# A two-block transformer kernel on one core: SBUF tiles of 1 KB and more moved to one byte offset, and the latents' squares added ahead of their sums

## The chip, the cores and the metric

The kernel runs on one core of a Trainium2 chip, as one program. The metric is the device time of one execution in microseconds (us). Before the change three runs took 1204.91, 1205.18 and 1206.57 us; the median is 1205.18 us.

## The reference, cut to what matters

256 tokens of width 1024, batch 1, all in float32, pass through two blocks one after the other:

```python
# first block
h = h + gated_deltanet(rmsnorm(h))            # 16 value heads of 128, chunks of 64
h = h + conv_gated_mlp(rmsnorm(h))            # "ffn 0": 1024 -> 2*2816 -> 1024
h = h + sliding_window_sink_attention(...)    # 16 heads of 64, window 128
h = h + conv_gated_mlp(rmsnorm(h))            # "ffn 1"
x = rmsnorm(h)
# second block, the "mixer" and "ffn 2"
proj = rms_norm(x) @ w_in
h_q, h_k, h_v, h_g, h_a, c_q, c_kv, k_pe = split(proj)
y_a = gla_branch(h_q, h_k, h_v, h_g, h_a) @ w_o_gla        # gated linear attention
y_b = mla_branch(rms_norm(c_q), rms_norm(c_kv), k_pe) @ w_o_mla   # latent attention
x = x + rms_norm((g_a * y_a + g_b * y_b) @ w_out)
x = x + rms_norm((silu(h @ w_gate) * (h @ w_up)) @ w_down)
```

In the mixer c_kv has 256 and c_q 384 columns; both are called latents here. Each is scaled by the reciprocal root of its mean square, so the sum of its squares over the columns is needed. The gate of gla_branch is log_sigmoid(h_a @ w_a2 + b), summed along the time of a chunk.

## The kernel before, in words

**A product in three parts.** Activations lie transposed in SBUF: 128 features on the partitions, 256 tokens along the free axis, so that one tile of 128 features is 1 KB in a partition. For float32 accuracy every operand is split into a rounded part and a remainder ("hi" and "lo"; in the names `xh` and `xl`, `wh` and `wl`). `mm3` (L248 to L252) makes a product of three matmuls: hi by hi (L250), lo by hi (L251), hi by lo (L252). In `gemm` the weights are stationary (128 x 128) and the activations stream past (256 columns, 1 KB a partition). In `gemm_nat`, and in the last product of ffn 2, it is the other way round: 128 tokens of an activation are stationary and 512 columns of the weights stream (2 KB a partition). In a row of the profile the operand ahead of the comma streams and the one behind it is stationary: `pb<-xh,wh` streams `xh`.

**Weights.** All weights lie in one array in the order in which they are used, in chunks of 128 x 1024. `w` (L231) hands out tiles of 128 columns; for each chunk `_prep` (L176) starts the DMA into `wr`, lets ScalarE round it into `wh` (L187) and VectorE subtract that to give `wl` (L188). One chunk feeds 24 matmuls that stream 256 columns.

**Order.** The program is written out by Python generators. A stage that is waiting for other engines is a "side" generator; each group of four weight tiles gives every side one step (`tick`), and `yield` puts off what follows by one step. So a number of yields is a distance in weight tiles between two pieces of a stage. The engines work through their queues in order.

**Where tiles lie.** Pools are laid one behind the other in a partition: constants, the weight pool `wp` (four buffers each of wr, wh, wl), `h`, the small pool `sp`, then `xp` with the pair xh, xl, then pools of the single stages. Within a pool tiles follow one another as they are first asked for, so that a tile begins where the small tiles ahead of it happen to end.

**The latents in the mixer.** `lat` (L1336) splits one of the five latent tiles and squares it on ScalarE (L1342) into a buffer `sql[i]`. `lat_stage` (L1431) waits until the two squares of c_kv exist, yields three times, adds them on VectorE (L1436), and at once issues the sum over the partitions (`colsum`, L367, a matmul with a column of ones); from that comes the scale `rkv`, which `rows` (L453, `rowp`) spreads over the partitions. For c_q it does the same with three squares (L1444, L1445), three yields and a second colsum. `la_stage` (L1391) runs beside it: it turns the rotary key (L1381, `rot`), makes the gate (L1404, in two halves), its logarithm on ScalarE (L1409 to L1411) and its running sum on VectorE (L1413 to L1421). `evac_kd` (L1460) scales the keys and multiplies them by that (L1467); their transposes stand on TensorE (L1473, `kdt`).

Of the kernel before, what the change touches and what calls it, by code (L numbers as in the profile page):

```python
# [2 lines left out]

# [1 line left out]

# [4 lines left out]
F32 = mybir.dt.float32  # L10
F32R = mybir.dt.float32r
BF16 = mybir.dt.bfloat16
I32 = mybir.dt.int32
AF = mybir.ActivationFunctionType
ALU = mybir.AluOpType
# [4 lines left out]
P = 128  # L20
# [87 lines left out]

CW = _cw_terms()

WARM = (5, 1, 3)
# [29 lines left out]
class Builder:  # L143
# [413 lines left out]
    def run(self):  # L557
        nc, tc = self.nc, self.tc
        with ExitStack() as es:
            self.cp = es.enter_context(tc.tile_pool(name="cp", bufs=1))  # L560
            self.wp = es.enter_context(tc.tile_pool(name="wp", bufs=2))
            self.hp = es.enter_context(tc.tile_pool(name="hp", bufs=1))
            self.sp = es.enter_context(tc.tile_pool(name="sp", bufs=2))
            self.xp = es.enter_context(tc.tile_pool(name="xp", bufs=1))
            self.dp = es.enter_context(tc.tile_pool(name="dp", bufs=1, space=DRAM))
            self.ps = es.enter_context(tc.tile_pool(name="ps", bufs=8, space=PSUM))
            self.h = self.hp.tile([P, KD, T], F32, name="h")
            self.cols = self.cp.tile([P, NCOL], F32, name="cols")
            self.ident = self.cp.tile([P, P], F32, name="ident")
            for b in range(4):  # L570
                nc.sync.dma_start(self.h[:, 2 * b : 2 * b + 2], self.a["xT"][:, 2 * b : 2 * b + 2])
            nc.sync.dma_start(self.ident, self.cst("ident"))
            self._raw(0)
            nc.sync.dma_start(self.cols, self.a["cols"])
            self.ones = self.cp.tile([P, P], F32, name="ones")
            nc.gpsimd.memset(self.ones, 1.0)
            self.gdn()
            if self.upto < 2:
                return
            with tc.tile_pool(name="xp2", bufs=1) as self.xp2:  # L580
                self.ffn(0)
                if self.upto < 3:
                    return
                self.swa()
            if self.upto < 4:
                return
            with tc.tile_pool(name="lp", bufs=1) as self.lp:
                self.block2_consts()
                self.ffn(1)
                if self.upto < 5:  # L590
                    return
                self.block2()
# [6 lines left out]
    def gdn(self):  # L599
        nc, tc, sp = self.nc, self.tc, self.sp  # L600
        x = self.newx()
        self.sqs = []
        with tc.tile_pool(name="gp", bufs=1) as gp:

            wb = self.bank("warm")
            warm = lambda n, r: [nc.tensor.matmul(wb[:, 0 : r.shape[1]], self.ones, r, start=True, stop=True) for _ in range(n)]
            warm(WARM[0], self.ones)
            for b in range(4):
                self.add_sq(self.sqs, "sqa", b, lambda o: nc.scalar.activation(o, self.h[:, 2 * b : 2 * b + 2], AF.Square))
            cs = self.colsum(self.sqs)  # L610
            if PRE0:
                self._prep(0)
            rc = self.rstd(cs, D)
            warm(WARM[1], self.sqs[0])
            rb = self.rows(rc, psum=True)
            warm(WARM[2], self.h[:, 0])
            for i in range(8):
                t = gp.tile([P, T], F32, tag="t2", bufs=8, name="xn")
                op = nc.vector.scalar_tensor_tensor(t, self.h[:, i], self.col("a_norm", i), rb, ALU.mult, ALU.mult)
                nc.scalar.activation(x[0][:, i], t, AF.Copy)  # L620
                nc.vector.tensor_tensor(x[1][:, i], t, x[0][:, i].bitcast(F32), ALU.subtract)  # L621
                if i in PINS:
                    self.pins[PINS[i]] = op
                    self._prep(PINS[i])
            self.gdn_body(gp, x)
# [407 lines left out]
    def ffn(self, layer):  # L1033
        nc, tc, sp = self.nc, self.tc, self.sp
        x = self.x
        self.stats_rows(D)
        with tc.tile_pool(name=f"fp{layer}", bufs=1) as fp:
            padded = [fp.tile([P, 2, 2 + T], F32, tag=f"fpad{i}", name=f"fpad{i}") for i in range(3)]
            for t in padded:
                nc.gpsimd.memset(t[:, :, 0:2], 0.0)  # L1040
            acts = {}
            self.side(self.bias_rows(fp) if layer == 0 else self.rope_tables(fp))

            def evac(g, bank):
                u = padded[g % 3]
                nc.vector.tensor_tensor(u[:, :, 2:], bank.rearrange("p (a t) -> p a t", a=2), self.bc2(self.rb), ALU.mult)
                y = fp.tile([P, 2, T], F32, tag="fy", bufs=2, name="fy")
                for i in range(2):
                    ct = g + NFF * i
                    w = lambda j: self.col(f"fcw{layer}", ct * 3 + j)  # L1050
                    nc.scalar.activation(y[:, i], u[:, i, 2:], AF.Identity, bias=self.col(f"fcb{layer}", ct), scale=w(2))
                    for j in range(2):
                        nc.vector.scalar_tensor_tensor(y[:, i], u[:, i, j : j + T], w(j), y[:, i], ALU.mult, ALU.add)  # L1053
                nc.scalar.activation(y[:, 0], y[:, 0], AF.Silu)
                nc.vector.tensor_tensor(y[:, 1], y[:, 1], y[:, 0], ALU.mult)
                ah = fp.tile([P, T], F32R, tag="ah", bufs=LAG + 1, name="ah")
                al = fp.tile([P, T], F32R, tag="al", bufs=LAG + 1, name="al")
                self.split(ah, al, y[:, 1])
                acts[g] = (ah, al)

            cts = []
            for g in range(NFF):
                cts += [g, g + NFF]
            self.acc_started = None
            up = self.gemm(f"w_up{layer}", x, KD, cts, evac, ko=KO[layer])
            for g in range(NFF):
                next(up)
                if g >= LAG and g - LAG not in acts:
                    self.settle()
                if g == LAG - 1:  # L1070
                    self.acc_open()
                if g >= LAG:
                    self.acc_k(f"w_dn{layer}", g - LAG, acts.pop(g - LAG))
            ks = list(range(NFF - LAG, NFF))
            if layer == 0:
                xa, xb = self.newx(), self.newx(tag="f", pool=self.xp2)
                self.x = (xa, xb)
                ev = self.boundary_evac([(xa, self.col("kvn", 0, 8)), (xb, self.col("bn", 0, 8))])
            else:
                wfp = self.sp.tile([P, 8], F32, tag="wfp", bufs=1, name="wfp")  # L1080
                nc.vector.tensor_tensor(wfp, self.col("fin", 0, 8), self.col("prem", 0, 8), ALU.mult)
                xa = self.newx(tag="x")
                self.x = xa
                ev = self.boundary_evac([(xa, wfp)], self.col("fin", 0, 8))
            self.acc_last(f"w_dn{layer}", ks, [acts.pop(k) for k in ks], ev)
        self.out_dbg(f"hf{layer}", self.h)
# [17 lines left out]
    def swa(self):  # L1104
        nc, tc, sp = self.nc, self.tc, self.sp
        xk, xq = self.x
        self.stats(D)
        with tc.tile_pool(name="sw", bufs=1) as ap:
            self.swa_body(ap, xk, xq)

    def swa_body(self, ap, xk, xq):
# [137 lines left out]

    def block2(self):  # L1250
        nc, tc, sp = self.nc, self.tc, self.sp
        with tc.tile_pool(name="mp", bufs=1) as mp:
            xm = self.mixer(mp)
        self.ffn2(xm)

# [34 lines left out]
    def mixer(self, mp):  # L1290
        nc, sp = self.nc, self.sp
# [41 lines left out]
        sql = [None] * 5  # L1333
# [97 lines left out]
        def lat_stage():  # L1431
            while sql[1] is None:
                yield
            for _ in range(3):
                yield
            nc.vector.tensor_tensor(sql[0], sql[0], sql[1], ALU.add)  # L1436
            c = self.colsum(sql[0:1])
            nc.vector.tensor_tensor(rkv, self.rstd(c, 256, rc), rc, ALU.mult)
            yield
# [3 lines left out]
                yield  # L1443
            nc.vector.tensor_tensor(sql[2], sql[2], sql[3], ALU.add)  # L1444
            nc.vector.tensor_tensor(sql[2], sql[2], sql[4], ALU.add)  # L1445
            for _ in range(3):
                yield
            c = self.colsum(sql[2:3])
            nc.vector.scalar_tensor_tensor(rqs, self.rstd(c, 384, rc), 192 ** -0.5, rc, ALU.mult, ALU.mult)
# [1 line left out]

        self.side(la_stage())
        self.side(lat_stage())
        list(self.gemm("w_c", x, KD, [4, 0, 1, 2], evac_c))

# [284 lines left out]
    def ffn2(self, xm):  # L1740
        nc, tc, sp = self.nc, self.tc, self.sp
        stt = nc.vector.scalar_tensor_tensor
        with tc.tile_pool(name="f2", bufs=1) as fp:
            wrow = fp.tile([P, 2, D], F32, tag="wrow", name="wrow")
            nc.gpsimd.dma_start(wrow, self.a["wrow"].to_broadcast([P, 2, D]))
            mw = fp.tile([P, 2, D], F32, tag="mw", name="mw")
# [269 lines left out]
```

## Time and profile before

| | |
|---|---|
| runs, us | 1204.91, 1205.18, 1206.57; median 1205.18 |
| the profiled execution, us | 1206.04 |
| its span, first to last instruction, us | 1204.2 |
| mean granted TensorE clock | 0.99 |
| TensorE matmuls busy | 1166.8 us, 97% of the span, 9308 instructions |
| TensorE weight loads busy | 1102.7 us, 92% |
| VectorE busy | 896.5 us, 74% |
| ScalarE busy | 689.4 us, 57% |
| DMA | 206.00 MB, 171 GB/s on average |

The profiled execution took 1206.04 us, 1.8 us more than its span of instructions. PE in the profile is TensorE at its matmuls and PEld at its weight loads; DVE is VectorE, ACT ScalarE. The ends of matmuls are modelled and overlap, so that the length of one matmul (0.28 us here) is no measure of its price; the distance from one start to the next is.

### The profile page before, as it was taken

The page shows a single profiled execution, that of the slowest core. Times are in us where ns is not written, and L with a number is a line of the kernel's source. Part 1 is how long each engine was busy: PE and PEld are TensorE (multiplying, and loading weights), DVE is VectorE, ACT ScalarE, POOL GpSimd, SP SyncE. Part 2 cuts the span into 40 slices and gives each one's busy share as a digit, 9 for nine tenths or more (in the row PEclk, how much of TensorE's full clock was granted, in tenths as well). Part 3 has the DMA queues.
Part 4 walks back from the last instruction along what each step waited for, and adds up shares of the span by engine and source line. Part 5 has one row for each costly group of instructions (what it writes and reads, how often), then busy time and mean ns, then how long its engine had stood idle before and what let it go on. Part 6 is the DMA issues. An engine that isn't in the chain of part 4 may idle for free.

```text
span 1204.2 us, 23264 instructions
## 1 busy us (share of the span) xinstructions
PE 1166.8 (97%) x9308; PEld 1102.7 (92%) x9308; DVE 896.5 (74%) x1645; ACT 689.4 (57%) x1172; POOL 24.7 (2%) x46
## 2 busy tenths in 40 slices
PE   6999999999999999989999999799999999999997
PEld 6989888999999999889999998689789998999996
DVE  5968977669877879879987879546666667665565
ACT  4786556546655556656655557546465555444443
POOL 2000000000000001000000000000000000000000
PEclk9999999999999999999999999799999999999999
DMA  6546375455665657435656555244245664566562
GB/s 211 191 134 202 120 224 179 140 164 164 218 191 190 187 189 244 132 101 172 196 190 192 183 186 177 70 156 142 88 150 184 192 216 153 174 191 188 185 192 86
DMA packets 68204, 206.00 MB, mean 171 GB/s; under 512 B 18085, under 2 KB 18229, under 8 KB 67840
## 3 DMA queue, kind: packets, MB, share of 16 engines
q1 hardware_dynamic: 65488, 194.77, 51.3%
q0 software_dynamic: 2608, 9.75, 2.3%
q8 instruction: 73, 1.20, 0.4%
q14 instruction: 35, 0.29, 0.1%
HBM read 199.75 MB, written 4.74 MB: 170 GB/s over the span
## 4 chain that ended last, share of the span: by engine, by line
PE 81%; DVE 11%; ACT 3%; issue 2%; DMA 1%; SPq 0%; DVEq 0%; ACTq 0%; POOLq 0%
PE pb L250 18%; PE pb L251 18%; PE pb L252 18%; PE acc L250 6%; PE acc L252 6%; PE acc L251 6%; DVE wl L188 3%; DVE cy L705 1%; DMA NT<-s 1%; DVE TI L817 1%; DVE fst L815 1%; ACT wh L187 0%; DMA ident<-cst 0%; ACT S L1178 0%; DVE fy L1053 0%
## 5 line engine op out<-in xcount | busy, mean ns | idle before, releaser
L188 DVE TENSOR_TENSOR wl<-wr,wh 128x1024 fp32r<-128x1024 f32 x362 | 441.9, 1223 | 193.7 <-ACT wh L187 192.8
L187 ACT ACTIVATE wh<-wr 128x1024 fp32r<-128x1024 f32 x362 | 381.7, 1057 | 319.6 <-issue 88.2
L250 PE MATMUL pb<-xh,wh 128*128 128x256 f32 x1224 | 346.4, 283 | 0.6 <-ACT xh L620 0.6
L251 PE MATMUL pb<-xl,wh 128*128 128x256 f32 x1224 | 343.1, 280 | 0.3 <-DVE xl L621 0.2
L252 PE MATMUL pb<-xh,wl 128*128 128x256 f32 x1224 | 342.8, 281 | 0.2 <-DVE wl L188 0.2
L250 PEld LDWEIGHTS pb<-xh,wh 128*128 128x128 f32 x1224 | 231.2, 189 | 3.1 <-issue 1.6
L251 PEld LDWEIGHTS pb<-xl,wh 128*128 128x128 f32 x1224 | 231.3, 189 | 0.9 <-DVE xl L621 0.4
L252 PEld LDWEIGHTS pb<-xh,wl 128*128 128x128 f32 x1224 | 231.0, 189 | 0.4 <-DVE wl L188 0.4
L250 PE MATMUL pb<-fh,wh 128*128 128x256 f32 x416 | 116.9, 282 | 0.0
L251 PE MATMUL pb<-fl,wh 128*128 128x256 f32 x416 | 116.1, 279 | 0.5 <-DVE fl L471 0.4
L252 PE MATMUL pb<-fh,wl 128*128 128x256 f32 x416 | 115.8, 279 | 0.0
L252 PE MATMUL acc<-ah,wl 128*128 128x256 f32 x352 | 98.1, 279 | 0.4 <-DVE wl L188 0.4
L251 PE MATMUL acc<-al,wh 128*128 128x256 f32 x352 | 98.2, 279 | 0.0
L250 PE MATMUL acc<-ah,wh 128*128 128x256 f32 x352 | 98.1, 279 | 0.0
L251 PEld LDWEIGHTS pb<-fl,wh 128*128 128x128 f32 x416 | 78.3, 188 | 1.5 <-DVE fl L471 0.8
L250 PEld LDWEIGHTS pb<-fh,wh 128*128 128x128 f32 x416 | 78.1, 188 | 1.3 <-issue 0.4
L252 PEld LDWEIGHTS pb<-fh,wl 128*128 128x128 f32 x416 | 78.2, 188 | 0.0
L1053 DVE SCALAR_TENSOR_TENSOR fy<-fpad,cols,fy 128x256 f32<-128x256 f32 x176 | 73.4, 478 | 0.0
L250 PE MATMUL pb<-wh,xh 128*128 128x512 f32 (+1 forms) x176 | 70.9, 405 | 0.0
L251 PE MATMUL pb<-wl,xh 128*128 128x512 f32 (+1 forms) x176 | 68.9, 391 | 1.5 <-DVE wl L188 1.5
L252 PE MATMUL pb<-wh,xl 128*128 128x512 f32 (+1 forms) x176 | 68.5, 389 | 0.0
L252 PEld LDWEIGHTS acc<-ah,wl 128*128 128x128 f32 x352 | 66.2, 188 | 0.6 <-DVE wl L188 0.6
(455 smaller groups left out, 2082.0 us busy)
## 6 DMA issues: line engine op xcount, KB each, us to landing
wr<-wall SPq DMA_DIRECT2D x362, 512.0 KB, 3.8
wzd<-zt POOLq DMA_DIRECT2D x8, 256.0 KB, 2.8
wzog<-wzd POOLq DMA_DIRECT2D x4, 512.0 KB, 4.3
bias<-bd POOLq DMA_DIRECT2D x4, 512.0 KB, 6.8
h<-xT SPq DMA_DIRECT2D x4, 256.0 KB, 4.1
h<-xT POOLq DMA_DIRECT2D x1, 1024.0 KB, 7.8
wrow<-wrow POOLq DMA_DIRECT2D x1, 1024.0 KB, 9.4
out_dram<-mw SPq DMA_DIRECT2D x4, 256.0 KB, 2.0
```

Of the source, the lines that this page charges most:

```text
L187: nc.scalar.activation(hi, r, AF.Copy)
L188: i = nc.vector.tensor_tensor(lo, r, hi.bitcast(F32), ALU.subtract)
L250: mm(out, ah, bh, start=start, stop=False, skip_group_check=skip)
L251: mm(out, ah, bl, start=False, stop=False, skip_group_check=skip)
L252: mm(out, al, bh, start=False, stop=stop, skip_group_check=skip)
L705: nc.vector.scalar_tensor_tensor(y[:, i, n:], u[:, : T - n], w(j), y[:, i, n:], ALU.mult, ALU.add)
L815: nc.vector.tensor_tensor(tmp, NT[:, j, j + 1 :].unsqueeze(2).to_broadcast([P, m, j + 1]), TI[:, j, 0 : j + 1].unsqueeze(1).to_broadcast([ ...
L817: nc.vector.tensor_tensor(TI[:, j + 1 :, 0 : j + 1], TI[:, j + 1 :, 0 : j + 1], tmp, ALU.add)
L1053: nc.vector.scalar_tensor_tensor(y[:, i], u[:, i, j : j + T], w(j), y[:, i], ALU.mult, ALU.add)
```

## The change

Two things change. First, a class `Split` stands in for nine of the tile pools (`sp`, `xp`, and those of the stages): tiles under 1 KB go to a second pool of their own, and larger ones are rounded up to a multiple of 512 bytes, so that all of the larger ones in such a pool begin at the same byte modulo 512. A filler tile pads the small pool so that the next pool begins there too. Second, in `lat_stage` the squares of c_kv are added as soon as they exist, and four yields lie between that and their colsum; for c_q the three yields become four.

```diff
+LINE = 512
+class Split:
+    def __init__(self, big, small, nbufs):
+        self.big, self.small, self.nbufs, self.tags = big, small, nbufs, {}
+    def tile(self, shape, dtype, **kw):
+        item = 2 if dtype == BF16 else 4
+        n = math.prod(shape[1:])
+        if n * item < 1024:
+            self.tags[kw.get("tag", kw.get("name"))] = -(-n * item // 32) * 32 * kw.get("bufs", self.nbufs)
+            return self.small.tile(shape, dtype, **kw)
+        unit = LINE // item
+        m = -(-n // unit) * unit
+        if m == n:
+            return self.big.tile(shape, dtype, **kw)
+        t = self.big.tile([shape[0], m], dtype, **kw)[:, :n]
...
+    def fill(self, rest):
+        n = (rest - sum(self.tags.values())) % LINE
+        if n:
+            self.small.tile([P, n // 4], F32, tag="fill", bufs=1, name="fill")
+@contextmanager
+def split_pool(tc, name, bufs, rest=0):
+    with tc.tile_pool(name=name, bufs=bufs) as big, tc.tile_pool(name=name + "s", bufs=bufs) as small:
+        p = Split(big, small, bufs)
+        yield p
+        p.fill(rest)
...
-            self.sp = es.enter_context(tc.tile_pool(name="sp", bufs=2))
-            self.xp = es.enter_context(tc.tile_pool(name="xp", bufs=1))
+            self.sp = es.enter_context(split_pool(tc, name="sp", bufs=2, rest=192))
+            self.xp = es.enter_context(split_pool(tc, name="xp", bufs=1))
...
         def lat_stage():
             while sql[1] is None:
                 yield
-            for _ in range(3):
-                yield
             nc.vector.tensor_tensor(sql[0], sql[0], sql[1], ALU.add)
+            for _ in range(4):
+                yield
             c = self.colsum(sql[0:1])
...
             nc.vector.tensor_tensor(sql[2], sql[2], sql[4], ALU.add)
-            for _ in range(3):
+            for _ in range(4):
                 yield
             c = self.colsum(sql[2:3])
```

The other seven pools (`xp2`, `lp`, `gp`, `fp0` and `fp1`, `sw`, `mp`, `f2`) become `split_pool` in the same way. The pools of the constants, of the weights and of `h` stay as they were. In the built programs the operands of TensorE then begin at these bytes:

| tile | what it feeds | before, byte mod 512 | after, byte mod 512 |
|---|---|---|---|
| xh, xl; fh, fl | most `gemm`s; stationary in `gemm_nat` | 480 | 128 (640 mod 1024) |
| lath, yoh, goh and their lo parts | products of the mixer | 480 | 128 (640 mod 1024) |
| ah, al in ffn 0 | second product | 128 (mod 1024 too) | 128 |
| ah, al in ffn 1 | second product | 64 (576 mod 1024) | 128 |
| ah, al in ffn 2 | second product, stationary | 192 | 128 |
| oh, ol of the deltanet | w_out | 256 (768 mod 1024) | 128 |
| oh, ol of the window attention | w_o | 352 (mod 1024 too) | 128 |
| wr, wh, wl, four buffers each | all products | 448 | 448 |
| h | residual | 448 | 448 |

Weight tiles follow each other at 512 bytes inside a chunk, so they begin at 448 and 960 modulo 1024 by turns.

The new code moves the lines of everything below it down by 40: L250 to L252 become L290 to L292, L188 becomes L228, L367 becomes L407, L1436 becomes L1474, L1473 becomes L1513.

The order of instructions differs in the mixer only, apart from one small VectorE instruction (`bh<-cols`, 128 x 16) that moves to the start of the program, because its tile now lies where nothing was before. TensorE's queue around the first colsum (`sql` are the squares, `rot` the rotary key, `gate` a half of the gate) stood like this before:

```order
L252 MATMUL pb<-xh,wl_9315 128x256
L367 MATMUL csum<-ones,sql 128x1 x2
L250 MATMUL pb<-xh,wh_9345 128x256
...
L1381 MATMUL rot<-kpr,rotm 64x256
L1404 MATMUL gate<-ha,wa_9179 128x256 x2
...
L453 MATMUL rowp<-dg,ones 128x128 x2
L1404 MATMUL gate<-ha,wa_9179 128x256 x2
...
L367 MATMUL csum<-ones,sql 128x1 x2
...
L1473 MATMUL kdt<-ident,kd 128x128 x4
```

With the change it stands like this:

```order
L292 MATMUL pb<-xh,wl_9350 128x256
L290 MATMUL pb<-xh,wh_9380 128x256
...
L1421 MATMUL rot<-kpr,rotm 64x256
L1444 MATMUL gate<-ha,wa_9214 128x256 x2
L290 MATMUL pb<-xh,wh_9380 128x256
L291 MATMUL pb<-xl,wh_9380 128x256
L407 MATMUL csum<-ones,sql 128x1 x2
...
L1444 MATMUL gate<-ha,wa_9214 128x256 x2
...
L493 MATMUL rowp<-dg,ones 128x128 x2
...
L407 MATMUL csum<-ones,sql 128x1 x2
...
L1513 MATMUL kdt<-ident,kd 128x128 x4
```

The first colsum now stands behind nine matmuls of the next chunk, the rotation, the first half of the gate and two more matmuls; between it and the second half of the gate stand 10 product matmuls, then 18 up to `rowp`, 30 up to the second colsum and 27 up to the transposes. Before these numbers were, from the first colsum on, 9 up to the rotation, 15 up to `rowp`, and, behind the second half of the gate, 21 up to the second colsum and 51 up to the transposes.

VectorE's queue from the chunk ahead of the addition to the running sum of the gate, before:

```order
L188 TENSOR_TENSOR wl_9531<-wr_9407,wh_9530 128x1024
L1436 TENSOR_TENSOR sql<-sql 128x256
L471 SCALAR_TENSOR_TENSOR latl<-pb,cols,lath 128x256
L378 TENSOR_SCALAR rv<-csum,rc 128x1 x2
...
L1383 TENSOR_TENSOR ropet<-rot,cossin 64x256
...
L1438 TENSOR_TENSOR rkv<-rd,rc 128x2
...
L1449 SCALAR_TENSOR_TENSOR rqs<-rd,rc 128x2
L188 TENSOR_TENSOR wl_9630<-wr_9528,wh_9629 128x1024
L1413 SCALAR_TENSOR_TENSOR la<-la,e_9253 128x1024
...
L1467 TENSOR_TENSOR kd<-kd,e_9253 128x512 x2
```

and with the change:

```order
L228 TENSOR_TENSOR wl_9566<-wr_9443,wh_9565 128x1024
L1474 TENSOR_TENSOR sql<-sql 128x256
L511 SCALAR_TENSOR_TENSOR latl<-pb,cols,lath 128x256
L1423 TENSOR_TENSOR ropet<-rot,cossin 64x256
L418 TENSOR_SCALAR rv<-csum,rc 128x1
...
L1478 TENSOR_TENSOR rkv<-rd,rc 128x2
...
L228 TENSOR_TENSOR wl_9665<-wr_9563,wh_9664 128x1024
L1453 SCALAR_TENSOR_TENSOR la<-la,e_9288 128x1024
...
L1507 TENSOR_TENSOR kd<-kd,e_9288 128x512
...
L1489 SCALAR_TENSOR_TENSOR rqs<-rd,rc 128x2
```

On VectorE the addition keeps its place behind the same chunk's `wl`; the rotation's product now stands ahead of the work on the colsum, and the scale of c_q (`rqs`) moves behind the product of the keys with the gate.

## Rows read from the trace of the kernel before

**Rows 1.** The page: busy us by engine (share of the span), instructions.
```profile
PE 1166.8 (97%) x9308; PEld 1102.7 (92%) x9308; DVE 896.5 (74%) x1645; ACT 689.4 (57%) x1172; POOL 24.7 (2%) x46
```

**Rows 2.** Groups by line and shape: line, engine, op, names, shapes, count; busy us, mean ns.
```profile
L250 PE MATMUL pb<-xh,wh 128*128 128x256 f32 x1224 | 346.4, 283 | 0.6 <-ACT xh L620 0.6
L250 PE MATMUL pb<-fh,wh 128*128 128x256 f32 x416 | 116.9, 282 | 0.0
L250 PE MATMUL acc<-ah,wh 128*128 128x256 f32 x352 | 98.1, 279 | 0.0
L250 PE MATMUL pb<-wh,xh 128*128 128x512 f32 x160 | 66.2, 416 | 0.0
L250 PE MATMUL acc<-oh,wh 128*128 128x256 f32 x192 | 55.1, 291 | 2.0 <-ACT oh L467 2.0
L250 PE MATMUL acc<-wh,ah 128*128 128x512 f32 x88 | 34.4, 391 | 0.0
L250 PE MATMUL pb<-yoh,wh 128*128 128x256 f32 x64 | 17.9, 279 | 0.0
L250 PE MATMUL pb<-lath,wh 128*128 128x256 f32 x52 | 14.8, 285 | 0.0
```

**Rows 3.** Timeline of PE, end of ffn 0: start us, length us, what it does.
```profile
436.61 0.28 PE L250 MATMUL pb<-xh,wh 128*128 128x256 f32 x1
...
442.21 0.28 PE L250 MATMUL acc<-ah,wh 128*128 128x256 f32 x1
...
455.83 0.28 PE L250 MATMUL pb<-xh,wh 128*128 128x256 f32 x1
```

**Rows 4.** Timeline of PE, end of ffn 1.
```profile
713.40 0.28 PE L250 MATMUL acc<-ah,wh 128*128 128x256 f32 x1
...
727.64 0.28 PE L250 MATMUL pb<-xh,wh 128*128 128x256 f32 x1
```

**Rows 5.** Timeline of PE, w_out of the deltanet: two starts, 51 matmuls apart.
```profile
249.93 0.28 PE L250 MATMUL acc<-oh,wh 128*128 128x256 f32 x1
...
255.94 0.28 PE L250 MATMUL acc<-oh,wh 128*128 128x256 f32 x1
```

**Rows 6.** Windows, PE alone: length, busy (count), granted clock, DMA share, GB/s.
```profile
442.40:455.80 13.40, 13.40 (x120) 1.00 0.62 195
713.60:727.60 14.00, 14.00 (x120) 1.00 0.61 188
```

**Rows 7.** Timeline of PE, 512 columns streaming: mixer, then the end of ffn 2.
```profile
784.32 0.48 PE L250 MATMUL pb<-wh,xh 128*128 128x512 f32 x1
...
804.01 0.28 PE L250 MATMUL pb<-lath,wh 128*128 128x256 f32 x1
...
1185.65 0.39 PE L250 MATMUL acc<-wh,ah 128*128 128x512 f32 x1
...
1196.33 0.39 PE L252 MATMUL acc<-wh,al 128*128 128x512 f32 x1
```

**Rows 8.** Timeline of PE from the first colsum to the transposes; idle us before, in brackets.
```profile
749.27 0.98 PE L367 MATMUL csum<-ones,sql 128*128 128x1 f32 x4 [2.77 <-DVE sql L1436]
...
752.31 1.11 PE L1381 MATMUL rot<-kpr,rotm 64*64 64x256 f32 x2
...
755.35 0.58 PE L250 MATMUL pb<-xh,wh 128*128 128x256 f32 x1
...
759.57 1.13 PE L1404 MATMUL gate<-ha,wa 16*128 16x256 f32 x4
...
778.49 0.90 PE L1473 MATMUL kdt<-ident,kd 128*128 128x128 f32 x3 [8.73 <-DVE kd L1467]
```

**Rows 9.** Windows, all engines: length, PE, PEld, DVE, ACT, POOL busy (count), granted clock.
```profile
535.00:575.00 40.00, 39.72 (x337) 39.49 (x336) 39.06 (x75) 28.28 (x46) 0.64 (x4) 1.00 0.47 150
749.20:759.30 10.10, 10.03 (x37) 8.24 (x38) 4.40 (x23) 2.90 (x7) 0.00 (x0) 0.50 0.17 55
773.10:783.20 10.10, 4.71 (x13) 3.89 (x14) 4.75 (x7) 1.88 (x3) 0.00 (x0) 0.50 0.20 70
```

More of the change, by code (lines that the diff above doesn't have):

```diff
@@ L1 @@
 import math
-from contextlib import ExitStack
+from contextlib import ExitStack, contextmanager
 import numpy as np
@@ L109 @@
 CW = _cw_terms()
+LINE = 512
[13 more added lines that the diff above has]
+        t = self.big.tile([shape[0], m], dtype, **kw)[:, :n]
+        if len(shape) == 2:
+            return t
+        ax = "abc"[: len(shape) - 1]
+        return t.rearrange("p (" + " ".join(ax) + ") -> p " + " ".join(ax), **dict(zip(ax, shape[1:])))
+    def fill(self, rest):
[8 more added lines that the diff above has]
+        p.fill(rest)
 WARM = (5, 1, 3)
@@ L579, in run @@
                 return
-            with tc.tile_pool(name="xp2", bufs=1) as self.xp2:
+            with split_pool(tc, name="xp2", bufs=1) as self.xp2:
                 self.ffn(0)
@@ L586, in run @@
                 return
-            with tc.tile_pool(name="lp", bufs=1) as self.lp:
+            with split_pool(tc, name="lp", bufs=1) as self.lp:
                 self.block2_consts()
@@ L602, in gdn @@
         self.sqs = []
-        with tc.tile_pool(name="gp", bufs=1) as gp:
+        with split_pool(tc, name="gp", bufs=1) as gp:
             wb = self.bank("warm")
@@ L1036, in ffn @@
         self.stats_rows(D)
-        with tc.tile_pool(name=f"fp{layer}", bufs=1) as fp:
+        with split_pool(tc, name=f"fp{layer}", bufs=1) as fp:
             padded = [fp.tile([P, 2, 2 + T], F32, tag=f"fpad{i}", name=f"fpad{i}") for i in range(3)]
@@ L1107, in swa @@
         self.stats(D)
-        with tc.tile_pool(name="sw", bufs=1) as ap:
+        with split_pool(tc, name="sw", bufs=1) as ap:
             self.swa_body(ap, xk, xq)
@@ L1251, in block2 @@
         nc, tc, sp = self.nc, self.tc, self.sp
-        with tc.tile_pool(name="mp", bufs=1) as mp:
+        with split_pool(tc, name="mp", bufs=1) as mp:
             xm = self.mixer(mp)
@@ L1433, in lat_stage @@
                 yield
-            for _ in range(3):
+            nc.vector.tensor_tensor(sql[0], sql[0], sql[1], ALU.add)
+            for _ in range(4):
                 yield
-            nc.vector.tensor_tensor(sql[0], sql[0], sql[1], ALU.add)
             c = self.colsum(sql[0:1])
@@ L1742, in ffn2 @@
         stt = nc.vector.scalar_tensor_tensor
-        with tc.tile_pool(name="f2", bufs=1) as fp:
+        with split_pool(tc, name="f2", bufs=1) as fp:
             wrow = fp.tile([P, 2, D], F32, tag="wrow", name="wrow")
```

## The prediction

> **What bounds the kernel now.** First the engines: TensorE is at its matmuls for 97% of the span, VectorE for 74% [rows 1]. So time is gained where matmuls follow each other faster, or where PE waits. The length of a matmul in the profile is modelled; what counts is the distance between starts.
>
> Then the groups of matmuls [rows 2]. Each row stands for three lines alike (L250, L251, L252). With 256 columns streaming there are 3 x 1224 on x, 3 x 416 on f, 3 x 352 on ah (half in ffn 0, half in ffn 1), 3 x 192 on oh (128 in the deltanet, 64 in the window attention), and 3 x 64 on yoh, as many on goh, and 3 x 52 on lath. With 512 columns: 3 x 160 with x stationary, 3 x 88 with ah.
>
> [...] At the end of ffn 0, 48 matmuls on x take 442.21 - 436.61 = 5.60 us, **116.7 ns** each; right behind them 120 on ah take 13.62 us, **113.5 ns** each [rows 3, 6]. Same shape, same weights' buffers, same engines at work beside them. At the end of ffn 1 the same code takes 14.24 us for its 120 on ah, **118.7 ns** [rows 4, 6]. In w_out 51 on oh take 6.01 us, 117.8 ns [rows 5]. The streamed tile begins at byte 480 mod 512 for x, 128 for ah in ffn 0, 64 for ah in ffn 1, 256 for oh; the weights begin at 448 everywhere. Only the tile at 128 is fast. With 512 columns, 84 matmuls with x stationary at 480 take 19.69 us, 234.4 ns (gemm_nat has 96, 12 of them ahead of the second transposes); 47 with ah stationary at 192 take 10.68 us, 227.2 ns [rows 7], twice 113.6.
>
> Last the waits. PE is idle for 2.77 us ahead of the first colsum, until VectorE has added two squares, and for 8.73 us ahead of the transposes kdt, until the keys are multiplied by the gate [rows 8]. [...]
>
> **The change part by part.**
>
> *Streamed tiles to 128.* All streamed activations get the place of ah in ffn 0, against weights that stay at 448. I take 113.5 ns for all. x: 3672 x 3.2 ns = 11.8 us. f: 1248 x 3.2 = 4.0. yoh, goh, lath: 540 x 3.2 = 1.7. ah of ffn 1: 528 x 5.2 = 2.7. oh: 576 x 4.3 = 2.5. Together 22.7 us. Not all of it arrives. From 535 to 575 us VectorE is busy 39.06 of 40 us [rows 9] and becomes the bound: the gain of 337 matmuls, 1.1 us, goes. Some 120 between 749 and 770 us stand ahead of a chain on other engines: 0.4 us. PE is idle 37.4 us in all [rows 1], 11.5 of them the two waits above; in what is left in the deltanet and the attention a faster PE waits longer, for which I take off 1.0 (an estimate; its bounds are 0 and 3). That leaves **20.2 us**.
>
> [...]
>
> *Stationary activations to 128.* Weights stream from 448 as before. No row has this pair. If it is as good as 192, the 480 with x gain 7.2 ns each, 3.5 us, and the 264 with ah nothing. If it is as bad as 480, x gains nothing and ah loses 264 x 7.2 = 1.9 us. 128 is nearer to 192 than to 480; but the distance from the weights' place changes too, so I take half of the better end, **1.7 us**, and keep -1.9 and 3.5.
>
> *The squares.* VectorE's addition keeps its place behind wl and releases the colsum at 749.27 us [rows 8]. PE ran out of work 2.77 us before. Now 9 matmuls, the rotation, half of the gate and two more matmuls stand ahead of the colsum; in full clock that is some 11 x 0.117 us and, by half of the 3.0 us that rotation and gate take in the half clock (752.31 to 755.35 [rows 8]), 1.5 us: 2.8 us. PE comes to the colsum when the addition is done, and has not been idle. So the wait goes, 2.8 us, and with it the half clock behind it: in 10.1 us PE is busy for 10.03 [rows 9] with work that needs half of that, 5.1 us. The gate's halves come that much earlier, and the chain from them to kdt (logarithm on ACT, running sum on VectorE, three chunks of weights between) stays as long. kdt starts 7.9 us earlier. The wait ahead of it stays: 75 product matmuls lie between the second half of the gate and kdt now (72 before), 9 us, and the chain behind the gate takes 778.49 - 760.70 = 17.8 us in the trace [rows 8]. So the half clock there stays too. It now lasts 4.8 us beyond the start of kdt (778.49 to 783.2); with a shorter wait it may reach 1.8 us further, 0.9 us of work. **7.0 us**; bounds 0 (another wait takes its place) and 9.
>
> *The yield for c_q* moves its colsum to where its squares have long been added; it never made PE wait. Nothing; if that fails, the rival on the wait below. *bh* moves to the start, one small instruction on VectorE in a chain that PE waits for: 0.2 us lost. Other tiles of 1 KB move as well, but VectorE and ACT rows of one shape show no dependence on place; nothing.
>
> **Sum**: 20.2 + 1.7 + 7.0 - 0.2 = 28.7 us. The profiled execution took 1206.04 us, so 1177.3; it lies 0.9 above the median of the runs, so against that **1176.5 us**.
>
> **The rivals.**
>
> *A. Place does not matter; the distances have another cause.* For it: ah in ffn 0 stands in one place of the program, so that something else there might be good. Against it: ffn 1 runs the same code, with the tile elsewhere, 5.2 ns slower, and x in ffn 0 runs beside the same evacuations. Left are the squares: 1205.2 - 7 = 1198 us. [...]
>
> *B. Slower: the pattern repeats after 1024 bytes, not 512.* x, f and most others now begin at 640 mod 1024, which no streamed tile had; it is 64 from ah of ffn 1 (576, the slowest) and 512 from the fast one. At 118.7 ns the 5460 matmuls on x, f, yoh, goh and lath lose 2.0 ns each, 10.9 us, the stationary ones 1.9; less 7.0 for the squares the kernel takes 1211 us. It is slower from the point where the distance on x rises by more than 7.0 / 5460 = 1.3 ns, to above 118.0. Against it: at the end of ffn 0 the weights begin at 448 and 960 mod 1024 by turns, and the mean of 113.5 leaves no room for one of them being slow.
>
> *C. The wait moves on.* PE may wait at rowp or at the second half of the gate, in whose way VectorE now has the rotation's product, and the clock may fall all the same. Then the squares give nothing: 1183.5 us. Against it: after the colsum PE has 10, then 18 matmuls, 3.2 us, and the gate.
>
> *D. Half of the tiles profit* (a mixture of A and B): 10 us on the products, 0 to 1.7 on the stationary ones, 5 on the squares: 1189 us.
>
> **How the numbers follow.** The forecast has 70%, A 8%, B 5%, C 9%, D 6%, and 2% are for no change, by rivals that cancel. A difference under 0.2% (2.4 us) can't be told from none here. Faster by more: forecast, A, C, D, 93%. Slower: B, 5%. Same: 2%. The lower end has all of the products (22.7), 3.5 for the stationary ones, 9 for the squares and 2 for the other matmuls, that read tiles moved to 128 too: 37 us, 1168. The upper end takes in C and D: 1190. A and B, the 13%, stay outside.
>
> **What would show it.** Right: 48 matmuls on x in ffn 0 and f in ffn 2 in 5.45 us, all 120 on ah in ffn 1 in 13.6 us; no wait at the first colsum, one stretch at half clock instead of two in the mixer, a wait of 6 to 9 us left at kdt; in gemm_nat a distance of 227 to 234 ns. Wrong: x at 116.7 ns or more, or the clock at half ahead of the gate.

## The result and the profile after the change

The changed kernel took **1189.94 us** (median of four runs, 1189.38 to 1190.39) beside 1205.88 us for the kernel before: a ratio of 0.9865, 95% interval 0.9848 to 0.9882. The forecast was 1176.5 us in a range of 1168 to 1190, so the gain came, 16 us in place of 29. The time lies 0.06 us inside the range. Taken again later, the same kernel took 1186.4 us (four runs, 1181.85 to 1190.64; ratio 0.9846, 0.9819 to 0.9873). That spread belongs to the explanation and comes back below.

The page of the changed kernel, the row that answers to [rows 1]: TensorE's matmuls are 11.5 us shorter, VectorE and ScalarE as before. The profiled execution took 1190.36 us, its span was 1188.2.

```profile
PE 1155.3 (97%) x9308; PEld 1093.9 (92%) x9308; DVE 896.0 (75%) x1645; ACT 689.1 (58%) x1172; POOL 24.7 (2%) x46
```

The mixer first. The timeline of PE in the changed kernel, to be laid beside [rows 8] (start, length, what it does; in brackets the idle time before it):

```profile
742.39 0.64 PE L1421 MATMUL rot<-kpr,rotm 64*64 64x256 f32 x2
742.96 1.13 PE L1444 MATMUL gate<-ha,wa 16*128 16x256 f32 x4
...
744.36 0.50 PE L407 MATMUL csum<-ones,sql 128*128 128x1 f32 x4
...
746.04 1.13 PE L1444 MATMUL gate<-ha,wa 16*128 16x256 f32 x4
...
765.40 1.09 PE L1513 MATMUL kdt<-ident,kd 128*128 128x128 f32 x4 [8.49 <-DVE rky L395]
```

The wait of 2.77 us at the first colsum is gone, the rotation takes 0.64 us at a granted clock of 1.00 in place of 1.11 at 0.50, and the wait ahead of the transposes is as long as it was, 8.49 us. In the mixer one stretch at half clock, 0.50, is left. But there is a new one in the attention, which the kernel before did not have in its trace. Windows of the changed kernel (length, busy time with count for PE, PEld, DVE, ACT, POOL, granted clock, DMA share, GB/s):

```profile
759.40:769.60 10.20, 4.20 (x12) 3.56 (x13) 7.28 (x20) 1.88 (x3) 0.00 (x0) 0.50 0.33 103
517.10:523.90 6.80, 6.20 (x29) 6.20 (x30) 4.01 (x13) 1.53 (x4) 0.00 (x0) 0.50 0.29 96
```

Now the products. Windows of PE alone (length, busy time and count, clock, DMA share, GB/s); the first two lie in ffn 0, the next two in ffn 1, the last in the mixer's products on x and goh. A matmul still at work when a window opens is counted in it, so two have to be taken off each count. Kernel before:

```profile
300.00:350.00 50.00, 50.00 (x434) 1.00 0.65 209
380.00:430.00 50.00, 50.00 (x434) 1.00 0.60 190
580.00:620.00 40.00, 40.00 (x343) 1.00 0.69 219
650.00:700.00 50.00, 50.00 (x429) 1.00 0.60 189
925.00:955.00 30.00, 30.00 (x260) 1.00 0.61 192
```

Changed kernel:

```profile
300.00:350.00 50.00, 50.00 (x443) 1.00 0.66 212
380.00:430.00 50.00, 50.00 (x444) 1.00 0.61 196
580.00:620.00 40.00, 40.00 (x342) 1.00 0.67 209
650.00:700.00 50.00, 50.00 (x427) 1.00 0.61 190
925.00:955.00 30.00, 30.00 (x257) 1.00 0.61 188
```

In these windows of ffn 0 every matmul now follows the last by 50 us / 441 = 113.4 ns, x as well as ah, as forecast. It is not so from the start of ffn 0: there the distance is 117.8 ns, and it turns to 113.3 behind a small matmul that makes bias rows (L1138). In the timeline three distances take 0.35 us ahead of it and five take 0.56 us behind it:

```profile
285.81 0.28 PE L292 MATMUL pb<-xh,wl 128*128 128x256 f32 x1
...
286.16 0.28 PE L292 MATMUL pb<-xh,wl 128*128 128x256 f32 x1
286.37 0.81 PE L1138 MATMUL biasp<-oneh,tbl 33*16 33x384 f32 x2
...
287.59 0.28 PE L290 MATMUL pb<-xh,wh 128*128 128x256 f32 x1
...
288.15 0.28 PE L292 MATMUL pb<-xh,wl 128*128 128x256 f32 x1
```

In ffn 1, with the same code, the same bytes and the same clock, the distance is 50 / 425 = 117.6 ns (117.8 from start to start), and so is it in the mixer. Summed over the starts of all matmuls with 256 columns that lie under 128 ns apart, what exceeds 113.33 ns each was 23.9 us before and is 15.7 now:

| us above 113.33 ns each | before | after |
|---|---|---|
| ffn 0, behind the matmul of the bias rows | 3.36 | 0.02 |
| ffn 1 | 6.37 | 6.73 |
| mixer | 4.15 | 4.23 |
| ffn 2 | 3.58 | 1.12 |
| deltanet, start of ffn 0, attention | 6.45 | 3.62 |

So the tiles at byte 128 gave 8.2 us of the 20.2 that the forecast took for them. Most of the missing ones are those of ffn 1 and the mixer.

### The profile page after: what moved, and what is told of

It reads as the page before. It is cut to its first block, busy times and chain, and to the rows that moved or that the text cites. A ratio compares the mean times of both kernels' runs of the same rounds, so it can differ in the third digit from the quotient of the medians.

```text
span 1188.2 us, 23265 instructions
## 1 busy us (share of the span) xinstructions
PE 1155.3 (97%) x9308; PEld 1093.9 (92%) x9308; DVE 896.0 (75%) x1645; ACT 689.1 (58%) x1172; POOL 24.7 (2%) x46
## 4 chain that ended last, share of the span: by engine, by line
PE 83%; DVE 10%; ACT 3%; issue 2%; DMA 1%; SPq 0%; DVEq 0%; ACTq 0%; POOLq 0%
PE pb L290 18%; PE pb L291 18%; PE pb L292 18%; PE acc L290 7%; PE acc L292 6%; PE acc L291 6%; DVE wl L228 3%; DVE cy L745 1%; DVE TI L857 1%; DVE fst L855 1%; DVE fy L1093 1%; DMA NT<-s 1%; ACT S L1218 0%; ACT wh L227 0%; PE pt L1251 0%
## 5 line engine op out<-in xcount | busy, mean ns | idle before, releaser
L228 DVE TENSOR_TENSOR wl<-wr,wh 128x1024 fp32r<-128x1024 f32 x362 | 441.7, 1223 | 185.3 <-ACT wh L227 184.4
L290 PE MATMUL pb<-xh,wh 128*128 128x256 f32 x1224 | 344.8, 282 | 0.3 <-ACT xh L660 0.3
L292 PE MATMUL pb<-xh,wl 128*128 128x256 f32 x1224 | 341.3, 279 | 0.2 <-DVE wl L228 0.2
L290 PEld LDWEIGHTS pb<-xh,wh 128*128 128x128 f32 x1224 | 230.5, 188 | 2.7 <-issue 1.3
L292 PEld LDWEIGHTS pb<-xh,wl 128*128 128x128 f32 x1224 | 229.9, 188 | 0.4 <-DVE wl L228 0.4
L290 PE MATMUL pb<-fh,wh 128*128 128x256 f32 x416 | 116.2, 280 | 0.0
L292 PE MATMUL pb<-fh,wl 128*128 128x256 f32 x416 | 115.1, 277 | 0.0
L292 PE MATMUL acc<-ah,wl 128*128 128x256 f32 x352 | 98.0, 279 | 0.2 <-DVE wl L228 0.2
L290 PE MATMUL acc<-ah,wh 128*128 128x256 f32 x352 | 98.0, 278 | 0.0
L290 PEld LDWEIGHTS pb<-fh,wh 128*128 128x128 f32 x416 | 78.1, 188 | 1.3 <-issue 0.4
L292 PEld LDWEIGHTS pb<-fh,wl 128*128 128x128 f32 x416 | 78.2, 188 | 0.0
L290 PE MATMUL pb<-wh,xh 128*128 128x512 f32 (+1 forms) x176 | 70.6, 403 | 0.0
L292 PE MATMUL pb<-wh,xl 128*128 128x512 f32 (+1 forms) x176 | 67.7, 385 | 0.0
L291 PEld LDWEIGHTS acc<-al,wh 128*128 128x128 f32 x352 | 66.8, 190 | 0.0
```

Of the source, the lines that this page charges most:

```text
L228: i = nc.vector.tensor_tensor(lo, r, hi.bitcast(F32), ALU.subtract)
L290: mm(out, ah, bh, start=start, stop=False, skip_group_check=skip)
L291: mm(out, ah, bl, start=False, stop=False, skip_group_check=skip)
L292: mm(out, al, bh, start=False, stop=stop, skip_group_check=skip)
```

## The experiments

**1. Places and interruptions by themselves.** The first kernel runs TensorE alone. It lays the streamed tile at each multiple of 32 bytes and starts each stretch behind another interruption.

```diff
+for x in range(0, 512, 32):
+    plan += [("run", x, 448, "c", 12), ("run", x, 448, "w128", 12), ("run", x, 448, "s", 12)]
+for kd in ("c", "o", "r", "s", "b", "f32", "f64", "f128", "f192", "f256", "w128", "w192", "w256", "w320", "w384", "c", "r"):
+    plan.append(("run", 128, 448, kd, 20))
```

> Computes nothing of the reference: TensorE alone runs stretches of mm3 (36 or 60 matmuls, 256 columns streaming) and of 512-column triples, each behind an interruption: two matmuls of one column, a 128x128 matmul, a 256-column matmul of ones, or a wait for a VectorE copy. The streamed tile begins at byte 0 to 480 mod 512 in steps of 32, the stationary one at 448, and then at others. Theory 1, the place alone: every stretch at 128 against 448 runs at 113.4 ns, those at 480 at 116.7, those at 64 at 118.6, whatever stands ahead of them. Theory 2, a state: at 128 against 448 a stretch runs at 113.3 or at 117.8 ns throughout, and which of the two depends on the interruption ahead of it, while at 480 it is 116.7 every time.

Seventeen stretches of 60 matmuls ran at 128 against 448, at full clock (a mean of 0.999 over the run): 7 at 113.3 ns and 10 at 117.8, by their mean from the eighth matmul on, within 0.3 ns but for one stretch with a pause in it. The six banks of PSUM that take the results in turn do not sort them: each has both values. Two of the seventeen stand behind the same interruption, a matmul of 256 columns with ones (L78). Windows of PE in them: 55 matmuls need 6.20 us in one and 6.00 in the other.

```profile
277.20:283.40 6.20, 6.20 (x55) 1.00 0.00 0
379.40:385.40 6.00, 6.00 (x55) 1.00 0.01 3
```

At 480 the five stretches had 116.6 to 116.7 ns. In these runs places count modulo 256: in the next experiment stretches whose two tiles lie at one byte, and stretches where they lie 256 bytes apart, all have 120.0 ns, and ffn 0 of the changed kernel has 113.4 ns with x at 640 mod 1024, so rival B has no ground. Theory 2 holds: a place can allow two distances, here 113.3 and 117.8 ns, and a stretch has one of them throughout; which one is called its **state** from here on. The kind of interruption alone does not choose it, as the two windows show.

**2. All pairs.** The same, over the places of both operands.

```diff
+for w in range(192, 448, 32):
+    for x in range(128, 384, 32):
+        for kd in ("s", "c", "w128"):
+            plan.append((x, w, kd, 0, 0))
+for d in range(32, 256, 32):
...
+        plan.append((128, 192, kd, 0, d))
```

> Computes nothing of the reference: stretches of 33 matmuls of mm3, as in the first such run, for all 64 pairs of places of the streamed tile and the stationary one in steps of 32 bytes over 256, each behind three interruptions (a 128x128 matmul, two matmuls of one column, a wait for VectorE); then, at 128 against 192, the lo tile of either operand moved by 32 to 224 bytes against its hi tile. In the first run the pattern came back after 256 bytes, and 113.3 ns came up only where the streamed tile lies 192 bytes behind the stationary one (mod 256), there beside 117.8. If the difference of the places decides, the 8 pairs with a difference of 192 all show both values. If one pair, or one offset between hi and lo, has 113.3 behind all three interruptions, that is a layout in which the state no longer matters.

Means over the last 12 distances of each stretch, by the place of the streamed tile less that of the stationary one, mod 256:

| difference | stretches | ns |
|---|---|---|
| 0, 96 | 48 | 120.0 |
| 32 (x before the change) | 24 | 116.67, twice 117.75 |
| 64 | 24 | 117.75 to 117.83 |
| 128, 160, 224 | 72 | 117.1 to 120.0 |
| 192 (x after the change) | 24 | ten times 113.33, 14 times 117.8 |

It is the difference that counts, not a byte: at 0, six of the eight pairs have both tiles at one byte, from 192 to 352, and two have them 256 apart, and all 24 stretches ran at 120.0 ns. Six of the eight pairs at a difference of 192 showed both values, two showed 117.8 ns three times. At 32, two stretches of 24 left 116.67 ns as well. With lo tiles of the weights moved away from their hi tiles, at a difference of 192 for these, 128 bytes gave 113.33 ns behind all three interruptions; 64 bytes gave 118.5, 118.2 and 118.5, the others 116.4 to 120.2. Moving the lo tile of the streamed operand gave 117.75 or more.

**3. Each part alone.** The new layout with the old order of the squares, and the reverse (the change's own diff, one half undone).

> The new layout with the old order of the squares. If the two parts add up, the wait ahead of the first column sum and the half clock behind it come back, and the kernel is 7.5 to 8 us above the changed one: 1197.5 us, 8 below the kernel before. If the squares gave nothing by themselves, 1190 us.

> The old layout with the new order of the squares. If the parts add up, 7.5 to 8 us below the kernel before: 1198 us, with one stretch at half clock in the mixer in place of two; product matmuls on x stay at 116.7 ns. If the squares gave nothing by themselves, 1205.5 us.

The squares alone: 1200.51 us (ratio 0.9939, 0.9924 to 0.9954; the kernel before took 1207.23 beside it), 6.7 us. The layout alone: 1192.59 us (1190.55 to 1198.19; ratio 0.9885, 0.9864 to 0.9907), 5 us less than parts that add up would have. Its trace tells why: ffn 1 ran at 113.3 ns there from 574 us on, by no difference in its program but by its state. Its 1584 matmuls follow each other at a mean of 115.1 ns, waits included, in place of 118.7 in the changed kernel; that is 5.7 us, and with these the parts add up. One of its windows, beside 427 in the changed kernel:

```profile
650.00:700.00 50.00, 50.00 (x444) 1.00 0.59 195
```

**4. An interruption put in on purpose.** ffn 0 has one small matmul that ffn 1 lacks, for the bias rows. The same was put into ffn 1 of the changed kernel, its result unread.

```diff
+    def kick(self):
+        for _ in range(12):
+            yield
+        b = self.bank("kick")
+        self.nc.tensor.matmul(b[0:16, 0:384], self.cols[0:33, 0:16], self.cols[0:33, 0:384], start=True, stop=True)
...
+            if layer == 1:
+                self.side(self.kick())
```

> The changed kernel with one more matmul in ffn 1, 33 x 16 against 384 columns, its result unread, as far behind the start of the stage as the matmul of the bias rows is in ffn 0. In the changed kernel ffn 0 went from 117.8 to 113.3 ns per matmul right behind that matmul, and ffn 1, without it, stays at 117.8 to 118 ns. Theory 2, a state that the interruption sets: the 1500 matmuls behind it go to 113.3 ns, 6.5 us less, 1183.5 us. Theory 1, ffn 1 is slower by something of its own in its places: nothing changes but 0.5 us for the extra matmul, 1190 us.

1184.44 us (1182.69 to 1189.52; ratio 0.9819, 0.9797 to 0.9840). Its timeline of PE shows the distance turn from 0.118 to 0.113 us behind L1135:

```profile
553.96 0.28 PE L291 MATMUL pb<-xl,wh 128*128 128x256 f32 x1
554.08 0.28 PE L292 MATMUL pb<-xh,wl 128*128 128x256 f32 x1
554.28 0.82 PE L1135 MATMUL kick<-cols 33*16 33x384 f32 x2
555.03 0.38 PE L290 MATMUL pb<-xh,wh 128*128 128x256 f32 x1
555.25 0.29 PE L291 MATMUL pb<-xl,wh 128*128 128x256 f32 x1
555.38 0.28 PE L292 MATMUL pb<-xh,wl 128*128 128x256 f32 x1
555.49 0.28 PE L290 MATMUL pb<-xh,wh 128*128 128x256 f32 x1
```

The windows of ffn 1 then hold 355 and 443 matmuls, where the changed kernel had 342 and 427:

```profile
580.00:620.00 40.00, 40.00 (x355) 1.00 0.65 217
650.00:700.00 50.00, 50.00 (x443) 1.00 0.61 195
```

**5. Its control.** The same extra matmul in the kernel before.

> The kernel before with the same extra matmul in ffn 1, so x at 480 and ah at 64. Theory 2: at these places there is one distance whatever comes ahead (116.7 on x, 118.6 on ah), so nothing changes but about 0.5 us for the matmul itself: 0 to 1 us above the kernel before. Rival: the extra matmul helps ffn 1 by something else, a pause that lets VectorE catch up, and then it helps here too, some 6 us.

1205.80 us, ratio 0.9995 (0.998 to 1.0009): nothing. Its window 650 to 700 us holds 428 matmuls (429 without the matmul). At the old places the same matmul changed no distance.

**6. The same interruption, put later.** The matmul of the bias rows in ffn 0, 60 steps later.

```diff
-        for _ in range(12):
+        for _ in range(72):
             yield
         b = self.bank("biasp")
```

> The changed kernel with the small matmul of the bias rows in ffn 0 put 60 steps later (72 yields in place of 12), nothing else. Theory 2: its interruption is what took ffn 0 to 113.3 ns, so the 720 matmuls that now come ahead of it stay at 117.8: 3.2 us slower than the changed kernel, 1193 us, unless a stall on the way changes the state as well. Theory 1, the place: ffn 0 stays at 113.3 ns from its start and the time stays at 1190 us.

The trace does what theory 2 says: 798 matmuls at 117.8 ns up to that matmul at 370 us, 113.3 behind it. Windows of its PE:

```profile
300.00:350.00 50.00, 50.00 (x427) 1.00 0.61 204
...
380.00:430.00 50.00, 50.00 (x443) 1.00 0.58 194
```

The time, 1188.52 us (1185.66 to 1191.50; ratio 0.9852, 0.9827 to 0.9877), can't be told from that of the changed kernel on the same chip (1186.4): 3 us is within the spread of either.

**7. The changed kernel again.**

> The changed kernel itself once more, on the chip of these runs. If the state of a stretch follows from the program, its trace shows ffn 0 at 113.3 ns and ffn 1 and the mixer at 117.8 to 118.4 again, and 1190 us; if it falls anew in every execution, the runs spread over 1180 to 1200 us and the trace shows another pattern. The 6.8 us at half clock in the attention, which the kernel with the extra matmul did not show, may come or not: 2 us.

Its profiled execution took 1181.85 us, and ffn 1 ran at 113.3 ns:

```profile
580.00:620.00 40.00, 40.00 (x355) 1.00 0.66 214
```

The program is the same. ffn 0 behind the bias rows, ffn 2 and the mixer came out as in the first profile (0.02, 1.11 and 4.25 us above 113.33 ns each), so of the long stages ffn 1 alone changed. The two profiles part in it at one wait for a weight tile. Timeline of PE in the first profile of the changed kernel:

```profile
572.78 0.28 PE L291 MATMUL acc<-al,wh 128*128 128x256 f32 x1
573.25 0.38 PE L292 MATMUL acc<-ah,wl 128*128 128x256 f32 x1 [0.20 <-DVE wl L228]
573.48 0.28 PE L290 MATMUL acc<-ah,wh 128*128 128x256 f32 x1
```

and in the second:

```profile
569.77 0.28 PE L291 MATMUL acc<-al,wh 128*128 128x256 f32 x1
570.24 0.39 PE L292 MATMUL acc<-ah,wl 128*128 128x256 f32 x1 [0.19 <-DVE wl L228]
570.46 0.28 PE L290 MATMUL acc<-ah,wh 128*128 128x256 f32 x1
```

Between the same two matmuls lie 474 ns in one and 470 in the other. Behind the first the 1296 matmuls that follow stay at 117.8 ns, behind the second nearly all go at 113.3: 1296 x 4.4 ns = 5.7 us. The length of the wait alone does not decide: in the traces of the layout alone and of the late bias rows the same two matmuls lie 475 and 472 ns apart, and the first goes on at 113.3 ns, the second at 117.8. The half clock in the attention did not come either; it came, for 3.4 or 6.8 us, in the layout alone and the squares alone among others, and not in the changed kernel with the extra matmul.

**8. Another difference.** All moved tiles at byte 0, 64 from the weights (mod 256).

```diff
-            self.sp = es.enter_context(split_pool(tc, name="sp", bufs=2, rest=192))
+            self.sp = es.enter_context(split_pool(tc, name="sp", bufs=2, rest=64))
```

> The changed kernel with all moved tiles at 0 mod 512 in place of 128 (the filler 128 bytes shorter), weights at 448: a difference of 64 mod 256. If the difference decides, every stretch with 256 columns runs at 117.8 ns, ffn 0 and ffn 2 too, which run at 113.5 in the changed kernel: 5935 matmuls x 4.4 ns = 26 us above 113.33 in place of 15.7, and 744 with 512 columns at 233.3 in place of 229.5: 10.5 + 2.8 us slower than the changed kernel, 1203 us. If one common byte was what helped, whichever it is, 1190 us.

1198.71 us (1195.77 to 1201.64; ratio 0.9939, 0.9914 to 0.9963), between the two. Its trace has ffn 0 at 113.3 ns behind the matmul of the bias rows, which no stretch by itself had shown at this difference, ffn 1 at 117.8 and ffn 2 at 117.9. Two of its windows:

```profile
300.00:350.00 50.00, 50.00 (x444) 1.00 0.63 208
...
650.00:700.00 50.00, 50.00 (x427) 1.00 0.58 184
```

So 64 allows two states as well, and the table of pairs is a sample, not a law.

**9. A layout without a choice.** Bytes between the weights' hi and lo tiles, with the tiles of the stages kept in their places.

```diff
         hi = self.wtile(j, F32R, "wh")
+        if j == 0:
+            self.wp.tile([P, 32], F32, tag="gap", bufs=1, name="gap")
         lo = self.wtile(j, F32R, "wl")
...
-            self.sp = es.enter_context(split_pool(tc, name="sp", bufs=2, rest=192))
+            self.sp = es.enter_context(split_pool(tc, name="sp", bufs=2, rest=64))
```

The first try had 16 columns, 64 bytes (and `rest=128`):

> The changed kernel with 64 bytes put between the weights' hi tiles and their lo tiles (wl then at 0 mod 512, wh stays at 448) and everything behind kept in its place, x at 128. In the pairs run this offset was the only one with 113.33 ns behind all three interruptions. If that carries over, ffn 1 and the products on yoh, goh and lath, which run at 117.8 to 118.4 ns in the changed kernel, go to 113.3: in its trace the matmuls with 256 columns lie 15.7 us above 113.33 ns each, some 2.5 of which (start of the kernel, the two extra weight tiles of ffn 2) stay, so 13 us less: 1177 us. If the state of the run sets the distance here as before, 1190 us. The products with 512 columns have another distance between their places too; up to 3 us more or 1 less from these.

That expectation rested on a row read wrongly: the pairs were listed by the place of the lo tile, 64, which is 128 bytes from the hi tile at 192. 64 bytes stood there with 118.2 to 118.5 ns, and the kernel did just that: 118.2 to 118.5 ns in every stage, 1208.31 us (1205.99 to 1210.90; ratio 1.0013, 1.0001 to 1.0025). Then 128 bytes:

> The changed kernel with 128 bytes between the weights' hi and lo tiles (wh 448, wl 64 mod 512, so 192 and 64 mod 256), all else as in the changed kernel. The run with 64 bytes had 118.2 ns in every stretch, which is what the pairs run has for 64 (118.0 to 118.5); its expectation took the wrong row. The row with 113.33 ns behind all three interruptions is the one with 128 bytes. If the pairs run carries over, every stretch with 256 columns goes to 113.3 ns whatever came ahead: of the 15.7 us that the changed kernel's matmuls lie above that, some 13 go: 1177 us. If a state remains, ffn 1 or the mixer stay at 117.8 ns: 1183 to 1190 us.

**1181.15 us** (1180.06 to 1183.39; ratio 0.9791, 0.9770 to 0.9811), faster than both kernels. Windows of its PE in ffn 0, ffn 1 and the mixer:

```profile
300.00:350.00 50.00, 50.00 (x444) 1.00 0.64 213
...
580.00:620.00 40.00, 40.00 (x355) 1.00 0.65 219
650.00:700.00 50.00, 50.00 (x444) 1.00 0.58 193
...
925.00:955.00 30.00, 30.00 (x267) 1.00 0.59 194
```

Above 113.33 ns each, 3.9 us are left of 15.7, most of them in the stages with many interruptions. And the old order of the squares in this layout:

> The kernel with 128 bytes between hi and lo weights and with the old order of the squares: the squares' worth where no state blurs it. By the trace of the changed kernel they gave 7.9 us between the first and second matmul behind them; so 1181 + 7.9 = 1189 us, with two stretches at half clock in the mixer. If some of that gain was the state's, 1184 to 1187 us.

1188.23 us (1187.76 to 1192.78; ratio 0.9858, 0.9836 to 0.9880): 7.1 us above the median with the new order, 8.1 us by the two ratios to the kernel before, for the two kernels ran at different times and on different chips. Its first colsum waits again and in the mixer the clock falls twice:

```profile
740.97 0.93 PE L409 MATMUL csum<-ones,sql 128*128 128x1 f32 x4 [2.77 <-DVE sql L1478]
```

```profile
741.00:751.00 10.00, 10.00 (x38) 8.18 (x38) 4.29 (x23) 2.95 (x7) 0.00 (x0) 0.50 0.15 53
765.00:775.00 10.00, 4.75 (x13) 3.89 (x14) 4.62 (x6) 1.89 (x3) 0.00 (x0) 0.50 0.17 57
```

## Why the prediction was right in sign and too large

*Streamed tiles to 128, 20.2 us: the step that failed.* It took 113.5 ns for all, because the one row at 128 was fast [rows 3, 6], and concluded "Only the tile at 128 is fast". Place and speed were one case each. What the runs showed in its place: at 128 against 448 a stretch runs at 113.3 or at 117.8 ns, and keeps to it, over up to 1296 matmuls, until something interrupts it; at 480 it ran at 116.7 in all long stretches. So the change trades 116.7 for either. ffn 0 came as forecast (3.3 us of 3.4), ffn 2 nearly (2.5 of 3.4), ffn 1 lost 0.4 where 5.0 were expected (1056 x 3.2 ns on x and 528 x 5.2 on ah, less 1.1 us), the mixer gained nothing where 3.8 were (1194 x 3.2), and the deltanet, the start of ffn 0 and the attention gave 2.8 of the rest, some 5. In all 8.2 us, and in the second profile, where ffn 1 runs at 113.3 ns, 5.7 more.

At one shape and full clock (1.00 in the windows of the kernels, a mean of 0.999 in the two runs of TensorE alone) the distance was 113.3 to 120.0 ns, by the difference between the places of the operand that streams and the stationary one. How the places act on it, no run shows.

*Stationary activations, 1.7 us: right.* In gemm_nat 84 matmuls now take 790.30 - 770.97 = 19.33 us, 230.1 ns in place of 234.4; in ffn 2 47 take 10.76 us, 228.9 in place of 227.2 [rows 7]. Over all starts x gained 1.4 us and ah stayed as it was. Timeline of PE in the changed kernel:

```profile
770.97 0.48 PE L290 MATMUL pb<-wh,xh 128*128 128x512 f32 x1
...
790.30 0.28 PE L290 MATMUL pb<-lath,wh 128*128 128x256 f32 x1
...
1169.50 0.39 PE L290 MATMUL acc<-wh,ah 128*128 128x512 f32 x1
...
1180.26 0.40 PE L292 MATMUL acc<-wh,al 128*128 128x512 f32 x1
```

*The squares, 7.0 us: right in size and in nearly each step.* No wait at the first colsum, full clock through rotation and gate, a wait of 8.49 us left at kdt (6 to 9 forecast). The row puts that wait down to rky, a step of the scale of c_q; the product of keys and gate that kdt reads ended at 765.25 us, 0.1 us ahead of it. One and the same product matmul, the last ahead of the first colsum in the old order, starts at these times in the kernel before and in the changed one:

```profile
746.22 0.27 PE L252 MATMUL pb<-xh,wl 128*128 128x256 f32 x1
```

```profile
741.17 0.28 PE L292 MATMUL pb<-xh,wl 128*128 128x256 f32 x1
```

From there to kdt the kernel before took 778.49 - 746.22 = 32.27 us [rows 8] and the changed kernel 765.40 - 741.17 = 24.23: 8.0 us less, 0.1 of it by shorter distances. Undone in the layout without a choice it was 7.1 us by the medians and 8.1 by the ratios. The 0.9 us that the forecast took off for a half clock that reaches 1.8 us further is a term that no row and no run shows. It did not come: the half clock (0.50) lasted 4.2 us beyond the start of kdt (765.40 to 769.6) in place of 4.8; the 0.6 us between them gave, as an estimate, 0.3 us more. The yield for c_q made PE wait nowhere, as said. Its work on VectorE now runs between the parts of the gate's chain, and that chain took 765.40 - 747.17 = 18.2 us in place of 17.8, so it can have cost 0.4 us at most. Rival C, 1183.5 us, fell: the clock was full, 1.00, ahead of the gate.

*bh, -0.2 us:* the first product started 0.8 us earlier, not later. That start lay at 15.3 to 16.1 us in the other profiles, so no gain is claimed from it.

*Other tiles of 1 KB, nothing:* two rows bear it out. VectorE's split `al<-fy,ah`, 128x256, took 422 ns in ffn 0 (tile at 128) and 423 in ffn 1 (at 64) in the kernel before, and 423 with both at 128; ScalarE's `ah<-fy` took 416, 418 and 417.

*The waits, -1.0 us:* in the attention the clock fell to 0.50 for 6.8 us, and 1.9 us were lost there. The forecast's 1.0 us was for a faster PE that waits longer, and not for this. It is no property of the change: the second profile of the same kernel has none, and the old layout with the extra matmul has 3.4 us of it.

Summed up for the profiled execution: 8.2 + 1.4 + 8.2 (the squares without the products) + 0.8 - 1.9 = 16.7 us, and the spans differ by 1204.2 - 1188.2 = 16.0; the 0.7 us between the two are not accounted for. That the range to 1190 holds the time is luck: its upper end was set by rivals C and D, and neither came as it was described. Rival D named 1189 us, the time that came, but for another reason: not half of the tiles profit, but some of the stretches, and whether ffn 1 is one of them changed from one execution to the next. Rival A fell with ffn 0 on x, rival B with the period of 256.

## What to carry to other kernels

A fast row is no rule until the same pair of places has been seen in a second stretch: here ah in ffn 0 was fast by its byte and by the stretch it stood in, for in ffn 1 the same byte gave 117.8 ns. Where matmuls of one shape show several distances between starts, a small kernel that runs the pairs of places behind several interruptions shows in one run which layouts are a choice; it can miss one, as at a difference of 64. With the tiles at 128, 128 bytes between the hi and lo weights were then worth another 5 us (1186.4 to 1181.15) to 9 us (1189.94 to 1181.15). And a kernel whose time spreads by several us over runs of one program wants two profiles before a stage is explained.

## What was not expected of the hardware

- Matmuls of 256 columns have, at full clock, a distance that depends on the places of streamed and stationary operand mod 256: 113.3 to 120.0 ns. At differences of 192 (alone and in the kernel) and 64 (in the kernel) two values are stable, 113.3 and 117.8, over up to 1296 matmuls, x and ah alike; at 32, two stretches of 24 ran at 117.8 in place of 116.67.
- A small matmul of 33 x 16 against 384 columns took stretches from 117.8 to 113.3 all six times that it stands at these places in the kernels (five traces); waits of 470 and 475 ns did so too, waits of 472 and 474 ns did not. What sets the state inside TensorE stays open, and so does why 128 bytes between hi and lo weights left only the shorter distance in all long stretches.
- The clock fell to half, 0.50, in the attention for 6.8 us in one execution of the changed kernel and not at all in the other. In the first the two longest waits of PE there were 1.8 and 1.1 us; in the kernel before, with 2.0 and 0.9 us, the clock stayed at 1.00.
